# A pair of modulation units on the second value unit, and a ScalarE copy ahead of the gMLP's norm

## The chip, the cores and the metric

The kernel is one program on one of the eight cores of a Trainium2 chip. A core has five engines with a queue each: TensorE (PE, with its weight loads shown apart as PEld), VectorE (DVE), ScalarE (ACT), GpSimd (POOL) and SyncE (SP). Here SP issues nearly all transfers, and POOL and ACT issue a few. The metric is device time in microseconds (us), the median of several runs.

## The reference, cut to what matters

One encoder layer is run on 1024 frames of a new stream and 32 frames of a running one, so 1056 rows of 1024 features. Everything is float32. In outline:

```
mod = silu(c) @ w_ada + b_ada                  # sh1, sc1, g1, sh2, sc2, g2
h   = x * (1 + sc1) + sh1
mq mk mv mo mi mf | fq fk fv ff | gu gv = split(h @ w_in)
hm  = mLSTM(mq, mk, mv, mi, mf), normed, times sigmoid(mo)
hf  = forgetting attention(fq, fk, fv, ff)
vn  = layer_norm(gv, gmlp_ln_g, gmlp_ln_b)      # over 256 features
hg  = gu * (tril(ws) @ vn + bs)
x   = layer_norm(ALPHA * x + (1 + g1) * (concat(hm, hf, hg) @ w_o))
h   = x * (1 + sc2) + sh2
x   = layer_norm(ALPHA * x + (1 + g2) * ((silu(h @ w_gate) * (h @ w_up)) @ w_down))
```

The outputs are y, the attention's k, v and log forget values, the mLSTM's final states, and for the running stream `vn`. Two things matter here: the columns of `mod` (the adaLN modulation, a product of one vector with a 1024 x 6144 matrix) and `vn`.

## The kernel before, in words

**Arithmetic.** A float32 product is made of three fast ones: each operand is split into a rounded part (`hi`) and the rest (`lo`), and TensorE forms hi·hi, hi·lo and lo·hi. The split of a weight tile is a copy on ScalarE (line 117) and a subtraction on VectorE or GpSimd (line 118). A weight tile of 512 KB comes into one of three `raw` buffers.

**The adaLN units.** `w_ada` is cut into 24 units of 256 columns, two loads of 512 KB each. `ada_parts` (lines 193 to 215) takes a list of units. For each it issues 8 narrow matmuls (four k-tiles in four row groups, two halves), which the chip's trace shows as 16 records; the units of one list use different rows of the same accumulation. Then, once for a list, there is one ScalarE copy of the bank (line 206, tile `ada_adas`), two transposes (line 211) and one VectorE reduction (line 213); and for each unit the two or three small VectorE operations of `ada_end`. Units 16 to 19 make g1, which is first read when the output projection is evacuated, far later.

Units 0 to 7 are worked in the first stage. Units 16 and 17 are worked as a list of two by `group`: their four loads go into the pool `pe` (tag `early`, `EB` = 4 buffers), and their work is put after the first row tile of the second value unit. Units 18, 19 and then 8 to 15 are in the list `rest`, which `more(n)` works off singly, with the pool `pl` (tag `late`, 2 buffers, so the two loads of a unit wait until the unit before has been read). `T1[3]` = 2 says that two of them, 18 and 19, are put after the first part of the gates; each `a` in the string `ORDER` takes one more.

**The value units.** `tm_unit` (line 389) multiplies all rows with 264 or 256 columns. It first does the 32 sample rows (`sample_tile`, line 409), then eight tiles of 128 rows, each of 24 matmuls (lines 402 to 404) into one of the three banks of the pool `pg` (tag `g`). The evacuation of a value tile is `evac_v`: a ScalarE copy from the bank to `traw` (line 434, two buffers), a store of it to `o_v` by SP, VectorE copies and a split into `vhl` (lines 437 to 441, two buffers), and a store of that to `dv` by SP. A bank is free once its line 434 has run, and that waits until the store from the same `traw` buffer, two tiles back, has landed.

**The gMLP's gate tiles.** In `ORDER`, `G0` and `G2p` are `tm_unit` on the gv columns, for row tiles 0 to 3 and 4 to 8, with `evac_gv` (line 468) for each tile; `G1p` and `G3` are the gu columns with `evac_gmlp`. `evac_gv` reads the bank twice on VectorE: for the statistics (lines 472, 473) and, after the reciprocal root (`rstd`: two ScalarE operations at lines 461 and 462, three VectorE ones at 464 to 466), for the normalising `tensor_scalar` (line 477) into `traw`. GpSimd then scales and shifts `traw` (lines 478, 479) and issues the store to `dvn`. A bank is held until line 477 is done.

**What sets the order.** The functions only list the work. A planner in the Tile framework puts it into the engines' queues by its own timeline: at each moment the earliest-listed instruction that is ready in that timeline goes first, so a load whose buffer is free is issued well ahead of its place in the code. Each queue then runs strictly in order. `tie` and `pinned` add order where the planner is not to choose; `group` ties TensorE's part of a list behind the last matmul before it. In the program, an SP transfer also waits for the eighth SP transfer before it, since eight completion semaphores are used in turn. Pools are laid out as a stack from both sides; `pe` lies on the right side, over memory that the first stage used and that `mx0` (the attention's, mLSTM's and gates' tiles) uses afterwards.

Of the kernel before, what the change touches and what calls it, by code (L numbers as in the profile page):

```python
# [7 lines left out]
F32 = mybir.dt.float32  # L8
# [7 lines left out]
P = 128  # L16
# [16 lines left out]
LWE = 1  # L33
NB = (3, 2, 2)
PRE = 5
EB = 4
T1 = (0, 0, 0, 2)
XB, AB = (3, 6)
HPA = 200
MLB = (1, 2, 3, 4, 5)  # L40
# [29 lines left out]
class Kernel:  # L70
# [396 lines left out]

    def evac_gv(self, tt, ps, n):
        nc = self.nc
        st = self.t(self.sm, [P, 6], F32, "bst", 2)  # L470
        mv = self.t(self.sm, [P, 2], F32, "bmv", 2)
        nc.vector.bn_stats(st[:n], ps[:n, :256])
        nc.vector.bn_aggr(mv[:n], st[:n])
        r = self.t(self.sm, [P, 1], F32, "brs", 2)
        self.rstd(r[:n], mv[:n, 1:2], self.eps5[:n], self.sm, "brt")
        v = self.t(self.sm, [P, 256], F32, "traw", 2)
        nc.vector.tensor_scalar(v[:n], ps[:n, :256], mv[:n, 0:1], r[:n], ALU.subtract, ALU.mult)  # L477
        nc.gpsimd.tensor_tensor(v[:n], v[:n], self.rowp[:n, 272:528], ALU.mult)
        nc.gpsimd.tensor_tensor(v[:n], v[:n], self.rowp[:n, 528:784], ALU.add)
        self.store(self.dvn[:n, tt, :], v[:n], nc.gpsimd)  # L480
        if tt == 8:
            self.store(self.d["o_vn"], v[:n])
# [1016 lines left out]
    def run(self):  # L1499
        nc, tc, d = self.nc, self.tc, self.d  # L1500
# [52 lines left out]
        sl = ExitStack()  # L1553
        self.pl = self.pada = self.pool("pl", ctx=sl)
        w1 = d["w_in_v"]
        rest = [18, 19] + list(range(8, 16))

        def more(n):
            for u in rest[:n]:
                self.ada((u,), self.pl, "late", 2, self.pt, "t")  # L1560
            del rest[:n]

        more(T1[0])
        se = ExitStack()
        pe = self.pool("pe", ctx=se, side="right")

        def group(units):
            def go():
                first = len(nc.cur_bb.bb.instructions)
                target = self.lastmm  # L1570
                for _ in self.ada_parts(units, raws, self.pt, "t"):
                    pass
                self.tie(nc.cur_bb.bb.instructions[first:], target, (mybir.EngineType.PE,))
                self.phase = "tm"
            raws = [self.ada_load(u, pe, "early", EB) for u in units]
            return go

        self.tm_unit(w1[0], 264, self.evac_v(0))
        self.tm_unit(w1[1], 264, self.evac_v(1), between={0: group((16, 17))})
        se.close()  # L1580
        s2 = ExitStack()
        self.mx = self.pool("mx0", ctx=s2)
        more(T1[2])
        gates = self.gates()
        next(gates)
        more(T1[3])
        self.foxbufs = (2, 2, 2, 2, 3)
# [278 lines left out]
```

## Time and profile before

| | |
|---|---|
| median of 3 runs | 1346.33 us (1344.91 to 1347.18) |
| the profiled execution: its time, its span | 1346.69 us, 1344.9 us |
| first stage (h and the first products) | 0 to 58 us |
| the two value units | 58 to 111 us |
| gates, heads, attention, mLSTM, gMLP | 111 to 345 us |
| the G0 and G2p tiles' norms | 263 to 279 us, 299 to 328 us |
| output projection, feed-forward, tail | 345 to 1345 us |

The profiled execution has 1.8 us around its span. A row of the timeline begins with its start and its length in us, then engine, source line, operation, written and read tiles; in brackets stands the idle time of the engine before it and what ended it. A row of the windows gives for each engine the busy us and in brackets the number of instructions, then the granted clock, the share of the DMA engines that was busy, and GB/s. A row of a source line gives the shortest, median and longest duration in ns.

### The profile page before, as it was taken

How to read it: one execution, taken by the hardware profiler on the slowest of the kernel's cores; microseconds unless marked ns; L12 is line 12 of the kernel's file. 1: busy time of each engine (PE TensorE's matmuls, PEld its weight loads, DVE VectorE, ACT ScalarE, POOL GpSimd, SP SyncE). 2: the span in 40 equal slices, each digit the busy share in tenths (PEclk: the TensorE clock that was granted, in tenths of full speed). 3: DMA queues.
4: the chain of work that ended last, by engine and by line, in shares of the span. 5: the costliest groups of instructions: out<-in, count | busy, mean ns of one | idle time of the engine just before them, and what ended most of it. 6: DMA issues, size and time to landing. Idle time of an engine off the chain costs nothing.

```text
span 1344.9 us, 25607 instructions
## 1 busy us (share of the span) xinstructions
PE 1324.0 (98%) x9684; PEld 1208.3 (90%) x9684; DVE 989.1 (74%) x2091; ACT 655.8 (49%) x1305; POOL 231.9 (17%) x263
## 2 busy tenths in 40 slices
PE   9999999999999999999999999999999999999996
PEld 6798888888999888888888888999999999999995
DVE  5635655678779667686876776678979887988777
ACT  3413445455547545545454454435754453635355
POOL 0102100143246100000000001464610000000341
PEclk9999999999999999999999999999999999999999
DMA  9585465546557754454344332663785858554221
GB/s 362 207 299 154 150 204 186 174 131 207 181 195 257 191 136 130 117 163 126 115 121 116 110 104 82 217 175 112 205 231 154 228 148 225 139 175 131 89 79 67
DMA packets 119450, 221.73 MB, mean 165 GB/s; under 512 B 18580, under 2 KB 62768, under 8 KB 119328
## 3 DMA queue, kind: packets, MB, share of 16 engines
q1 hardware_dynamic: 112096, 207.55, 49.0%
q0 software_dynamic: 6032, 11.94, 5.2%
q8 instruction: 76, 1.25, 0.4%
q10 hardware_dynamic: 1200, 0.62, 0.2%
q14 instruction: 46, 0.38, 0.1%
HBM read 188.13 MB, written 51.85 MB: 178 GB/s over the span
## 4 chain that ended last, share of the span: by engine, by line
PE 68%; DVE 4%; DMA 1%; ACT 1%; issue 1%; DVEq 0%; ACTq 0%
PE up_g L130 6%; PE up_g L132 6%; PE up_g L131 6%; PE dn_g L130 4%; PE dn_g L132 4%; PE dn_g L131 4%; PE sup_u L132 3%; PE sup_u L131 3%; PE sup_u L130 3%; PE wo_g L131 2%; PE wo_g L132 2%; PE wo_g L130 2%; PE sup_g L132 2%; PE sup_g L131 2%; PE sup_g L130 2%; PE fox_t L943 2%
## 5 line engine op out<-in xcount | busy, mean ns | idle before, releaser
L130 PE MATMUL up_g<-tm_ah,up_whi 128*128 128x512 f32 (+1 forms) x384 | 140.0, 365 | 0.0
L131 PE MATMUL up_g<-tm_al,up_whi 128*128 128x512 f32 (+1 forms) x384 | 140.0, 365 | 0.0
L132 PE MATMUL up_g<-tm_ah,up_wlo 128*128 128x512 f32 (+1 forms) x384 | 139.7, 364 | 0.0
L1368 ACT CAST sup_whi<-sup_raw 128x1024 fp32r<-128x1024 f32 x54 | 56.1, 1048 | 89.3 <-PE dn_u L131 43.9
L130 PEld LDWEIGHTS up_g<-tm_ah,up_whi 128*128 128x128 f32 x384 | 72.3, 188 | 11.1 <-DVE tm_al L1246 0.4
L132 PEld LDWEIGHTS up_g<-tm_ah,up_wlo 128*128 128x128 f32 x384 | 72.3, 188 | 11.1
L131 PEld LDWEIGHTS up_g<-tm_al,up_whi 128*128 128x128 f32 x384 | 72.3, 188 | 10.7
L916 ACT ACTIVATE fox_p<-fox_s,fox_fmx 128x384 f32<-128x384 f32 (+2 forms) x96 | 55.2, 579 | 53.0 <-DVE fox_fmx L914 41.2
L1199 DVE SCALAR_TENSOR_TENSOR wo_z<-dn_g,start_mod,wo_z 128x512 f32<-128x512 f32 (+4 forms) x120 | 60.3, 521 | 22.6 <-PE dn_g L132 22.0
L118 DVE TENSOR_TENSOR up_wlo<-up_raw,up_whi 128x1024 fp32r<-128x1024 f32 x50 | 65.2, 1305 | 15.0 <-ACT up_whi L117 13.7
L1369 DVE TENSOR_TENSOR sup_wlo<-sup_raw,sup_whi 128x1024 fp32r<-128x1024 f32 x54 | 68.0, 1263 | 10.7 <-ACT sup_whi L1368 10.7
L117 ACT CAST up_whi<-up_raw 128x1024 fp32r<-128x1024 f32 x50 | 52.4, 1048 | 47.2 <-PE up_g L131 23.9
L130 PE MATMUL dn_g<-up_acth,dn_whi 128*128 128x512 f32 (+2 forms) x200 | 73.5, 368 | 0.8 <-DVE wo_z L1199 0.8
L132 PE MATMUL dn_g<-up_acth,dn_wlo 128*128 128x512 f32 (+2 forms) x200 | 73.3, 366 | 0.0
L131 PE MATMUL dn_g<-up_actl,dn_whi 128*128 128x512 f32 (+2 forms) x200 | 72.8, 365 | 0.0
L948 ACT CAST fox_pth<-fox_t 128x512 fp32r<-128x512 f32 (+1 forms) x80 | 41.6, 542 | 59.2 <-PE fox_t L943 57.5
L117 ACT CAST dn_whi<-dn_raw 128x1024 fp32r<-128x1024 f32 (+1 forms) x44 | 42.7, 971 | 51.7 <-PE up_g L131 16.0
L911 DVE TENSOR_REDUCE fox_fmx<-fox_s 128x1 f32<-128x384 f32 (+2 forms) x96 | 52.8, 553 | 16.3 <-PE fox_s L908 15.0
L949 DVE TENSOR_TENSOR fox_ptl<-fox_t,fox_pth 128x512 fp32r<-128x512 f32 (+1 forms) x80 | 49.9, 631 | 15.9 <-ACT fox_pth L948 15.6
L118 DVE TENSOR_TENSOR dn_wlo<-dn_raw,dn_whi 128x1024 fp32r<-128x1024 f32 (+1 forms) x44 | 49.5, 1125 | 10.4 <-ACT dn_whi L117 9.5
L402 PE MATMUL tm_g<-tm_whi,start_h1h 128*128 128x256 f32 (+1 forms) x192 | 55.3, 288 | 0.7 <-DVE tm_traw L477 0.7
L1320 POOL DMA_DIRECT2D start_dp<-w_gu x19 | 19.8, 1067 | 209.0 <-DMA start_dp<-w_gu 209.0
(684 smaller groups left out, 4799.7 us busy)
## 6 DMA issues: line engine op xcount, KB each, us to landing
up_raw<-w_gu SPq DMA_DIRECT2D x50, 512.0 KB
ada_late<-w_ada SPq DMA_DIRECT2D x28, 512.0 KB
dn_raw<-w_dn SPq DMA_DIRECT2D x28, 512.0 KB
sup_raw<-w_gu SPq DMA_DIRECT2D x20, 512.0 KB
start_dp<-w_gu SPq DMA_DIRECT2D x19, 512.0 KB
start_dp<-w_gu POOLq DMA_DIRECT2D x19, 512.0 KB, 8.0
wo_raw<-w_o SPq DMA_DIRECT2D x18, 512.0 KB
sup_raw<-start_dp SPq DMA_DIRECT2D x18, 512.0 KB
```

The lines of the kernel that those rows point to most:

```text
L117: nc.scalar.copy(hi[:, :w], raw[:, :w])
L118: (eng or nc.vector).tensor_tensor(lo[:, :w], raw[:, :w], f(hi[:, :w]), ALU.subtract)
L130: nc.tensor.matmul(ps, hi, xh(k), start=start and k == 0, stop=False)
L131: nc.tensor.matmul(ps, hi, xl(k), start=False, stop=False)
L132: self.lastmm = nc.tensor.matmul(ps, lo, xh(k), start=False, stop=stop and k == n - 1)
L402: nc.tensor.matmul(ps[:, :ncol], xh, hi, start=k == 0, stop=False)
L911: nc.vector.tensor_reduce(mxs[:, x:x + 1], s[:, :w], AX.X, ALU.max, negate=True)
L916: nc.scalar.activation(pr[:, lo:hi], banks[x][:, :hi - lo], AF.Exp, bias=mxs[:, 0:1], accum_out=sums[:, x:x + 1])
L949: nc.vector.tensor_tensor(pl[:, :e], ps[:, :e], f(ph[:, :e]), ALU.subtract)
L1199: self.lastz = self.nc.vector.scalar_tensor_tensor(z[:, m, x:y], ps[:, x - a:y - a], g[i], z[:, m, x:y], ALU.mult, ALU.add)
L1368: nc.scalar.copy(h, x)
L1369: tt(l, x, f(h), ALU.subtract)
```

## The change

Two things are done. First, units 18 and 19 leave `rest` and become a list of two, like 16 and 17. Its loads are listed in the code right after the first pair's work, after the first row tile of the second value unit, and its work after that unit's sixth row tile (number 5). `EB` becomes 8, so that the second pair has four buffers of its own; `T1[3]` becomes 0. With that, `rest` begins at unit 8, and the two `late` buffers are first used by unit 8. Second, `evac_gv` takes its `traw` tile at the start; for row tiles 0 to 7 ScalarE copies the bank into it, and the statistics and the `tensor_scalar` read the copy; the `tensor_scalar` writes the copy in place. Tile 8 (the sample rows) is as before.

```diff
-EB = 4
-T1 = (0, 0, 0, 2)
+EB = 8
+T1 = (0, 0, 0, 0)
...
     def evac_gv(self, tt, ps, n):
         nc = self.nc
+        v = self.t(self.sm, [P, 256], F32, "traw", 2)
+        if tt < 8:
+            nc.scalar.copy(v, ps[:, :256])
+            ps = v
         st = self.t(self.sm, [P, 6], F32, "bst", 2)
...
         self.rstd(r[:n], mv[:n, 1:2], self.eps5[:n], self.sm, "brt")
-        v = self.t(self.sm, [P, 256], F32, "traw", 2)
         nc.vector.tensor_scalar(v[:n], ps[:n, :256], mv[:n, 0:1], r[:n], ALU.subtract, ALU.mult)
...
-        rest = [18, 19] + list(range(8, 16))
+        rest = list(range(8, 16))
...
         self.tm_unit(w1[0], 264, self.evac_v(0))
-        self.tm_unit(w1[1], 264, self.evac_v(1), between={0: group((16, 17))})
+        pairs = [group((16, 17))]
+        self.tm_unit(w1[1], 264, self.evac_v(1), between={
+            0: lambda: (pairs[0](), pairs.append(group((18, 19)))), 5: lambda: pairs[1]()})
```

## The prediction

> **What bounds the kernel.** I read the head of the page first, then the windows, then what TensorE waited for between 55 and 420 us, then the timelines around the changed places.
>
> ```profile
> span 1344.9 us, 25607 instructions
> PE 1324.0 (98%) x9684; PEld 1208.3 (90%) x9684; DVE 989.1 (74%) x2091; ACT 655.8 (49%) x1305; POOL 231.9 (17%) x263
> ```
>
> TensorE is busy 1324.0 of 1344.9 us, so nothing can win more than the 20.9 us in which it is not, plus work taken off it. The windows of the changed stages (busy us by engine, clock, DMA share, GB/s):
>
> ```profile
> 58.00:110.00 52.00, 51.21 (x545) 49.62 (x545) 18.31 (x66) 11.77 (x32) 0.00 (x0) 1.00 0.78 264
> 140.00:260.00 120.00, 118.90 (x1010) 104.02 (x1009) 73.31 (x201) 62.99 (x155) 4.22 (x7) 1.00 0.54 167
> 260.00:280.00 20.00, 19.45 (x142) 18.05 (x141) 14.23 (x33) 7.58 (x16) 11.15 (x13) 1.00 0.55 186
> 300.00:330.00 30.00, 28.30 (x275) 25.81 (x264) 25.38 (x80) 14.31 (x40) 12.87 (x19) 1.00 0.56 178
> ```
>
> TensorE lost 0.8 us in the value units, 1.1 in 120 us after them, 0.55 and 1.7 where the gate tiles' norms are. The waits name each loss (engine, line, releaser: total, times, longest):
>
> ```profile
> PE fox_o L951 <- DVE fox_ptl L949: 1.1, 1, 1.1
> PE tm_g L416 <- DVE tm_traw L477: 1.0, 1, 1.0
> PE tm_g L416 <- ACT tm_traw L434: 0.7, 1, 0.7
> PE tm_g L402 <- DVE tm_traw L477: 0.7, 1, 0.7
> PE tm_g L402 <- DVE tm_brt L464: 0.6, 1, 0.6
> ```
>
> Three of these are a bank held by the norm (L477 twice, and L464, an operation of the same chain), together 2.3 us. One, 0.7 us, is a bank of the value units that ScalarE had not yet copied. Every us won or lost here moves the end by a us, since TensorE is full afterwards.
>
> **Part 1, TensorE's work for units 18 and 19.** A single unit in the timeline of before (its matmuls, then its transposes), and the pair 16/17:
>
> ```profile
> 131.23 0.29 PE L130 MATMUL fm_g<-start_h1h,gates_whi 128*128 128x272 f32 x1
> 131.45 1.07 PE L202 MATMUL ada_t<-ada_late,start_c 128*32 128x256 f32 x16
> 132.45 0.40 PE L131 MATMUL fm_g<-start_h1l,gates_whi 128*128 128x272 f32 x1
> 132.68 0.28 PE L132 MATMUL fm_g<-start_h1h,gates_wlo 128*128 128x272 f32 x1
> ```
>
> ```profile
> 135.33 0.29 PE L132 MATMUL fm_g<-start_h1h,gates_wlo 128*128 128x272 f32 x1
> 135.46 0.38 PE L211 MATMUL ada_t<-start_ident,ada_adas 128*128 128x128 f32 x2
> 135.59 0.38 PE L130 MATMUL fm_g<-start_h1h,gates_whi 128*128 128x272 f32 x1
> 135.80 0.28 PE L131 MATMUL fm_g<-start_h1l,gates_whi 128*128 128x272 f32 x1
> ```
>
> ```profile
> 87.80 0.28 PE L404 MATMUL tm_g<-tm_whi,start_al 128*128 128x264 f32 x1
> 88.01 1.93 PE L202 MATMUL ada_t<-tm_early,start_c 128*32 128x256 f32 x32
> 89.88 0.39 PE L402 MATMUL tm_g<-tm_whi,start_ah 128*128 128x264 f32 x1
> 90.11 0.29 PE L403 MATMUL tm_g<-tm_wlo,start_ah 128*128 128x264 f32 x1
> ```
>
> Matmuls follow each other at about 0.13 us (135.33 to 135.46). From 131.23 to 132.68 are 1.45 us for two such steps and the unit's matmuls: 1.45 - 0.26 = 1.19. Its two transposes: 135.80 - 135.33 - 0.26 = 0.21. Two single units: 2 x 1.40 = 2.80. The pair: 90.11 - 87.80 - 0.26 = 2.05, plus one set of transposes 0.21 = 2.26. **Saved 0.54 us**, as much for the second change of tile shape as for the transposes. All of it is on the path, for TensorE has no pause around either place. The ScalarE copy and reduction saved (one each) are off the path, as is `ada_end`, whose count stays: g1 is read 200 us later. Bounds: 0.6 won; or 1.1 lost, if the single units were filling a gap at 131 and 141 us that a stall like fox_o's (1.1) takes. I take -0.54, the measured rows.
>
> **Part 2, the loads, and the value units' stores.** Here the change can cost. In SP's queue, loads are issued as soon as buffers allow:
>
> ```profile
> 68.35 1.29 SPq L87 DMA_DIRECT2D tm_early<-w_ada  x2
> 70.93 0.34 SPq L91 DMA_DIRECT2D o_v<-tm_traw  x1
> 71.32 1.19 SPq L87 DMA_DIRECT2D tm_early<-w_ada  x2
> 72.62 0.51 SPq L91 DMA_DIRECT2D start_dv<-tm_vhl  x1
> 73.19 1.23 SPq L87 DMA_DIRECT2D ada_late<-w_ada  x2
> 74.76 0.37 SPq L91 DMA_DIRECT2D o_v<-tm_traw  x1
> ```
>
> ```profile
> 76.46 0.38 ACT L434 COPY tm_traw<-tm_g 128x264 f32<-128x264 f32 x1 [4.68 <-DMA o_v<-tm_traw]
> 83.20 0.38 ACT L434 COPY tm_traw<-tm_g 128x264 f32<-128x264 f32 x1 [6.37 <-DMA o_v<-tm_traw]
> ...
> 84.46 0.38 ACT L434 COPY tm_traw<-tm_g 128x264 f32<-128x264 f32 x1
> ...
> 85.68 0.39 ACT L434 COPY tm_traw<-tm_g 128x264 f32<-128x264 f32 x1
> ```
>
> ```profile
> 80.24 0.29 DVE L440 CAST tm_vhl<-tm_traw 128x256 fp32r<-128x256 f32 x1 [3.20 <-DMA start_dv<-tm_vhl]
> 83.64 1.13 PE L416 MATMUL tm_g<-tm_raw,start_hs 128*32 128x66 f32 x64 [0.66 <-ACT tm_traw L434]
> ```
>
> The store issued at 74.76 stands behind six loads and lands at 83.2: 8.4 us, in which ScalarE's sixth copy waits, and TensorE for its bank. The rate: from the landing at 76.46 (store of 70.93) to the one at 80.24 (72.62) two 512 KB loads and a 256 KB store arrive, 1.31 MB in 3.8 us; a load is about 1.45 us.
>
> After the change, the pair 18/19 wants four loads and unit 8 two, as the two `late` buffers are free from the start; before, only unit 18's two were issued here. So four loads (5.8 us) are new in this stretch. Two of the pair's take the places of 73.19. For the other four loads I expect the next free places: one between the stores that follow 74.76 and the copy at 84.46, which moves to about 85.5, and three ahead of the store that the copy at 85.68 waits for, which moves to about 91. TensorE then waits for the bank of 84.46, +1.0, and begins the second unit's second tile at 90.9 instead of 89.88, where the bank of the last copy is 0.5 late: **+1.5 us** in all. Later copies have two tiles (5.8 us at 24 x 0.12) of slack, and the loads of v for the heads now wait for the second pair's memory, which eases the queue behind. The end below is -0.7 (the existing 0.66 goes too, if the stores land earlier), the end above +5.8 (all four ahead of the store of 74.76). I take +1.5, since a store that is ready precedes a load listed after it in the planner's order. The pair's work at tile 5, some 15 us after its last load, waits for nothing.
>
> **Part 3, the gate tiles.** Eight ScalarE copies are added, and eight VectorE operations change their source:
>
> ```profile
> L452 ACT COPY tm_traw<-tm_g x16: 362/372/376, 172.6 to 256.6; 128x256 f32<-128x256 f32 x16
> L477 DVE TENSOR_SCALAR tm_traw<-tm_g,tm_bmv,tm_brs x8: 528/544/545, 265.6 to 323.8; 128x256 f32<-128x256 f32 x8
> ```
>
> The copies are 8 x 0.372 = 3.0 us of ScalarE, which is busy 7.58 of 20 and 14.31 of 30 us there: hidden. VectorE's `tensor_scalar` may fall from 0.544 towards the 0.29 of the cast at 80.24, which reads and writes SBUF, 2 us at most, hidden too. What counts is when the bank comes free: after one copy, not after statistics, two ScalarE and five VectorE operations. Of the 2.3 us I take **-2.0**: a bank that the copy frees some us earlier isn't waited for, but the copies now hold `traw` (two buffers) from the copy until the store to `dvn` has landed, and a copy that waits for it stops ScalarE, and behind it the weight casts of line 117, for which the splits on VectorE and GpSimd and then TensorE's next unit wait. Those casts are what is late next. Bounds: -2.3 (all three waits) to +1.5 (three tiles' ScalarE stops of 0.5 us, the size of the waits that go).
>
> **The sum.** -0.54 + 1.5 - 2.0 = -1.0 us against the profiled execution's 1346.7: 1345.7. That execution is 0.4 above the median of the runs shown, so 1345.3 as a median, within 0.2% (2.7 us, about what a measurement of this kernel can tell from no change; its three runs spread over 2.3).
>
> **Rivals** (as medians).
> *Slower: all new loads ahead of the waiting store.* Place: between 71 and 76 us. If the planner puts the four before the store of 74.76, the copy of 83.20 comes at 89.0 and TensorE's 0.66 becomes 6.5: -2.54 + 5.8 = +3.3, 1349.6. It decides once all but a fraction of one load is ahead (5.2 us needed to pass +2.7). For it: nothing but buffers holds loads back; against: a ready store goes first.
> *Faster: the stores stay ahead.* Parts 1 and 3 whole and the 0.66 gone: -0.54 - 2.3 - 0.66 = -3.5, 1342.8; with the 0.66 kept, 1343.5. For it: DMA is busy only 0.78 of the stage.
> *The copy moves the wait.* ScalarE stalls on `traw` for as much as the bank wait was: part 3 is 0, sum +1.0, 1347.3.
> *The planner shifts the rest.* Between 110 and 260 us TensorE lost 1.1 us in one stall; other queue orders can hardly win there, but four new stalls of that size give +4.4 - 1.0 = +3.4, 1349.7.
> *VectorE is held by GpSimd.* Beside a weight split of GpSimd, a 0.16 us operation took 2.72:
>
> ```profile
> 273.33 2.72 DVE L465 SCALAR_TENSOR_TENSOR tm_brt<-tm_brt,tm_brs 128x1 f32<-128x1 f32 x1
> ```
>
> If two of the eight `tensor_scalar`, now from memory to memory, are held 2.5 us each and half of that reaches TensorE through the weight splits, -1.0 + 2.5 = +1.5, 1347.8. [...]
>
> **How the numbers follow.** The forecast 0.32; stores ahead 0.22; copy moves the wait 0.14; loads ahead 0.14; planner 0.13; held VectorE 0.05. The forecast's own range is 1343.8 to 1347.0. Faster by over 0.2%: 0.22 and a sliver of the forecast, 0.25. Slower: the two rivals at 1349.6 and 1349.7, 0.28 with the upper reaches of the others. Within: 0.47. The range reaches from the faster case's 1342.8 to past the slower ones, 1350.2.
>
> **What would show it.** Right: one 32-record group of units 18 and 19 near 107 us, and none near 131 and 141; TensorE's wait for L434 1 to 2 us at 84 to 91; no wait on L477 or L464; a wait of ScalarE for the `dvn` store. Wrong: a wait for L434 above 4 us, or none; TensorE idle over 2 us between 110 and 260; casts of line 117 in 265 to 330 that TensorE waits for; the new `tensor_scalar` above 1 us.

## The result, and the profile after

The changed kernel takes 1351.6 us against 1346.24 for the kernel before, 1.0040 times as long (95% interval 1.0031 to 1.0050); beside it on another chip 1350.85 against 1346.4, 1.0030 (1.0020 to 1.0041). The forecast was 1345.3, with a range to 1350.2: the change is slower, by 4.5 to 5.4 us, and beyond the range. Three executions of the kernels below, one each of e3_held, e8b_copy48 and e10_held_copy_act, took 1430, 7389 and 2162 us and are left out of every time, ratio and count. The changed kernel's profiled execution took 1353.02 us, 6.3 more than that of before. The head of its page:

```profile
span 1351.2 us, 25608 instructions
PE 1327.4 (98%) x9682; PEld 1211.6 (90%) x9682; DVE 988.6 (73%) x2090; ACT 658.5 (49%) x1312; POOL 228.9 (17%) x263
```

TensorE has two instructions less, and is busy 3.4 us *more*; its idle time grew by 2.9 (1351.2 - 1327.4 = 23.8, before 20.9). Fewer instructions that take longer point to the clock, the seventh column of the windows (busy us of PE, PEld, DVE, ACT, POOL, then clock, DMA share, GB/s):

```profile
82.00:88.00 6.00, 3.14 (x79) 2.76 (x78) 2.65 (x4) 3.02 (x7) 0.00 (x0) 0.96 1.03 412
88.00:94.00 6.00, 6.00 (x56) 4.92 (x55) 1.60 (x8) 0.87 (x3) 0.00 (x0) 0.75 1.03 411
140.00:260.00 120.00, 119.55 (x992) 105.69 (x991) 71.97 (x197) 61.59 (x151) 6.67 (x11) 1.00 0.53 161
260.00:280.00 20.00, 20.00 (x152) 18.16 (x152) 11.11 (x28) 8.51 (x19) 10.19 (x11) 1.00 0.58 178
300.00:330.00 30.00, 29.10 (x278) 26.38 (x276) 24.38 (x79) 15.66 (x47) 11.28 (x18) 1.00 0.57 185
330.00:340.00 10.00, 9.51 (x62) 8.02 (x61) 8.93 (x28) 7.36 (x22) 1.56 (x2) 0.83 0.94 284
380.00:390.00 10.00, 7.76 (x64) 7.42 (x63) 8.47 (x9) 3.24 (x5) 6.49 (x10) 1.00 0.58 194
```

The gate tiles' stretches won 1.35 us of the 2.0 forecast (0.55 lost in 260 to 280 is now 0; 1.70 in 300 to 330 is now 0.90), and between 140 and 260 us 0.45 is lost instead of 1.1. The value units lose 2.9 us in 82 to 88 (before 0.8) and then run six us at a mean clock of 0.75. And there are two losses where none was looked for: a low clock at 330 to 340 (0.83 over 10 us, 1.7 us), and 2.2 us at 380 to 390, in the output projection. The waits of TensorE in 55 to 420 us name them:

```profile
PE wo_g L130 <- DVE wo_z L1202: 2.5, 3, 1.2
PE tm_g L402 <- ACT tm_tmsum L420: 1.5, 1, 1.5
PE tm_g L416 <- ACT tm_traw L434: 1.3, 1, 1.3
PE mlstm_s L765 <- DVE tm_brt L465: 0.9, 1, 0.9
```

(Lines from 477 on stand three lower down than in the kernel before: L477 is L480, L1199 is L1202.) No wait for the norm's bank is left.

**In the value units**, this is SP's queue, and below it ScalarE's:

```profile
75.27 0.38 SPq L91 DMA_DIRECT2D o_v<-tm_traw  x1
76.47 0.33 SPq L87 DMA_DIRECT2D tm_early<-w_ada  x1
76.89 0.66 SPq L91 DMA_DIRECT2D start_dv<-tm_vhl  x1
79.27 0.33 SPq L87 DMA_DIRECT2D tm_early<-w_ada  x1
80.52 0.98 SPq L87 DMA_DIRECT2D ada_late<-w_ada  x2
82.46 0.34 SPq L91 DMA_DIRECT2D o_v<-tm_traw  x1
```

```profile
76.92 0.38 ACT L434 COPY tm_traw<-tm_g 128x264 f32<-128x264 f32 x1 [4.20 <-DMA o_v<-tm_traw]
84.14 0.38 ACT L434 COPY tm_traw<-tm_g 128x264 f32<-128x264 f32 x1 [6.84 <-DMA o_v<-tm_traw]
...
86.33 0.86 ACT L420 COPY tm_tmsum<-tm_g 32x66 f32<-32x66 f32 x4
90.72 0.38 ACT L434 COPY tm_traw<-tm_g 128x264 f32<-128x264 f32 x1 [3.53 <-DMA o_v<-tm_traw]
91.47 0.38 ACT L434 COPY tm_traw<-tm_g 128x264 f32<-128x264 f32 x1 [0.36 <-DMA o_v<-tm_traw]
```

The tile copied at 76.92 is stored only at 82.46, behind four loads. Its buffer is the one the copy of 90.72 needs: before, the copy in this place came at 84.46. So two of the three banks are held until 91, the second unit has only the sample tile's bank to go on with, and TensorE waits 1.5 us for that as well. The loads hold that store up chiefly in SP's queue. From the end of its copy (77.30) to its issue are 5.2 us, and for 3.5 of them SP waits for earlier loads to land before it can issue the next transfer; in before the store of this tile was issued at once (76.87). From issue to landing it then takes 8.3 us, in before at most 7.6.

What the clock then does is seen in the distance of matmuls and in windows of one us:

```profile
88.07 0.42 PE L403 MATMUL tm_g<-tm_wlo,start_ah 128*128 128x264 f32 x1
88.29 0.42 PE L404 MATMUL tm_g<-tm_whi,start_al 128*128 128x264 f32 x1
```

```profile
87.00:88.00 1.00, 0.76 (x4) 0.76 (x5) 1.00 (x1) 0.19 (x1) 0.00 (x0) 0.77 1.00 410
88.00:89.00 1.00, 1.00 (x7) 1.00 (x6) 0.72 (x4) 0.00 (x0) 0.00 (x0) 0.50 1.01 394
89.00:90.00 1.00, 1.00 (x6) 1.00 (x6) 0.00 (x0) 0.00 (x0) 0.00 (x0) 0.50 1.07 402
90.00:91.00 1.00, 1.00 (x7) 1.00 (x6) 0.00 (x0) 0.28 (x1) 0.00 (x0) 0.53 1.07 433
91.00:92.00 1.00, 1.00 (x12) 0.86 (x15) 0.83 (x4) 0.48 (x2) 0.00 (x0) 1.00 1.00 410
```

It is 0.22 us from one matmul to the next instead of 0.13, until 90.9. By the windows the clock is at one half for some 3.4 us; one minus the clock, summed over them, is 1.7 us. Such a stretch is called a fall below. Ahead of this one TensorE had two gaps, of 1.31 and 1.55 us, with 1.1 us of work between them.

**In the output projection**, rows of the timeline of before, and then of after:

```profile
371.62 0.50 DVE L492 SCALAR_TENSOR_TENSOR fm_qkl<-fm_g,start_qsc,fm_qkh 128x272 fp32r<-128x272 f32 x1 [1.69 <-DMA start_dql<-fm_qkl]
376.25 7.58 POOL L1193 TENSOR_TENSOR wo_z<-wo_z,wo_pv 128x256 f32<-128x256 f32 x7 [2.22 <-ACT wo_pv L1057]
378.46 0.45 DVE L1071 TENSOR_TENSOR wo_zs<-wo_z 128x256 f32<-128x256 f32 x1
```

```profile
377.49 1.22 DVE L118 TENSOR_TENSOR wo_wlo<-wo_raw,wo_whi 128x1024 fp32r<-128x1024 f32 x1 [3.05 <-ACT wo_whi L117]
378.63 0.49 DVE L495 SCALAR_TENSOR_TENSOR fm_qkl<-fm_g,start_qsc,fm_qkh 128x272 fp32r<-128x272 f32 x1
379.26 1.62 POOL L499 TENSOR_TENSOR fm_qkr<-fm_qkh,fm_qkl 128x272 f32<-128x272 f32 x1 [5.46 <-ACT wo_pv L1060]
381.90 4.89 POOL L1196 TENSOR_TENSOR wo_z<-wo_z,wo_pv 128x256 f32<-128x256 f32 x7
382.67 0.48 DVE L1202 SCALAR_TENSOR_TENSOR wo_z<-wo_g,start_mod,wo_z 128x256 f32<-128x256 f32 x1 [1.50 <-POOL wo_z L1196]
383.19 3.88 DVE L1074 TENSOR_TENSOR wo_zs<-wo_z 128x256 f32<-128x256 f32 x1
386.99 0.47 DVE L1202 SCALAR_TENSOR_TENSOR wo_z<-wo_g,start_mod,wo_z 128x256 f32<-128x256 f32 x1
```

The planner, with another list in front of it, has put the last early head's split (`fm_qkl`, one tile of 272 columns) behind a weight split, which itself waits 3.05 us for ScalarE's cast. GpSimd's addition for that head then comes after `wo_pv` is there instead of 4 us before it, and holds back the seven subtractions from z, which GpSimd does next: they begin 3.0 us after `wo_pv` was begun, in before 0.5. VectorE waits 1.5 us for the first of them. Then its sum of z takes 3.88 us instead of 0.45, until GpSimd is through; the evacuation behind it comes late, and TensorE waits for the bank. From the first to the last matmul of the output projection (rows of its tile in before and after):

```profile
L130 PE MATMUL wo_g<-tm_ah,wo_whi x128: 278/281/468, 366.9 to 413.8; 128*128 128x256 f32 x128
```

```profile
L130 PE MATMUL wo_g<-tm_ah,wo_whi x128: 277/281/469, 370.2 to 420.4; 128*128 128x256 f32 x128
```

46.9 us became 50.2. This length, "the projection's length" below, and TensorE's loss in 82 to 88 us tell in each experiment which of the two is there. The length is the surer sign: the loss in 82 to 88 varies from 0 to 2.74 in kernels that have before's loads.

### The profile page after: what moved, and what is told of

Its sections match the earlier page's. It is cut to its first block, busy times and chain, and to the rows that moved or that the text cites. A ratio compares the mean times of both kernels' runs of the same rounds, so it can differ in the third digit from the quotient of the medians.

```text
span 1351.2 us, 25608 instructions
## 1 busy us (share of the span) xinstructions
PE 1327.4 (98%) x9682; PEld 1211.6 (90%) x9682; DVE 988.6 (73%) x2090; ACT 658.5 (49%) x1312; POOL 228.9 (17%) x263
## 4 chain that ended last, share of the span: by engine, by line
PE 65%; DVE 4%; DMA 4%; ACT 2%; issue 2%; SPq 0%; POOL 0%; DVEq 0%; ACTq 0%; POOLq 0%
PE up_g L130 6%; PE up_g L132 6%; PE up_g L131 6%; PE dn_g L130 4%; PE dn_g L132 4%; PE dn_g L131 4%; PE sup_u L132 3%; PE sup_u L131 3%; PE sup_u L130 3%; PE wo_g L130 2%; PE sup_g L132 2%; PE sup_g L131 2%; PE wo_g L132 2%; PE wo_g L131 2%; PE sup_g L130 2%; PE fox_t L946 2%
## 5 line engine op out<-in xcount | busy, mean ns | idle before, releaser
L1202 DVE SCALAR_TENSOR_TENSOR wo_z<-dn_g,start_mod,wo_z 128x512 f32<-128x512 f32 (+4 forms) x120 | 60.1, 519 | 22.3 <-PE dn_g L132 21.6
L402 PE MATMUL tm_g<-tm_whi,start_ah 128*128 128x256 f32 (+1 forms) x192 | 55.7, 291 | 1.5 <-ACT tm_tmsum L420 1.5
```

Source lines behind the costliest of these rows:

```text
L402: nc.tensor.matmul(ps[:, :ncol], xh, hi, start=k == 0, stop=False)
L1202: self.lastz = self.nc.vector.scalar_tensor_tensor(z[:, m, x:y], ps[:, x - a:y - a], g[i], z[:, m, x:y], ALU.mult, ALU.add)
```

## The experiments

All ratios are to the kernel before on the same chip. "Clock low" counts the executions whose mean granted clock was 0.996 or less; of the kernel before that were 34 of 119. In the 17 profiled executions that mean is 0.997 or 0.998 where there is no fall ahead of the kernel's last 12 us, 0.996 where there is one (r_after, e4_late8held, e9_traw4, e13_after_act), and 0.995 with the two of the change.

| kernel | time, before (us) | ratio (95%) | TensorE lost in 82 to 88 | projection's length | clock low |
|---|---|---|---|---|---|
| the change | 1351.6, 1346.24 | 1.0040 (1.0031 to 1.0050) | 2.86 | 50.2 | 4 of 6 |
| r_after, the same again | 1350.85, 1346.4 | 1.0030 (1.0020 to 1.0041) | 2.08 | 50.0 | 6 of 7 |
| e1_pair | 1347.22, 1345.65 | 1.0013 (1.0002 to 1.0024) | 2.54 | 47.1 | 4 of 10 |
| e2_copy | 1348.81, 1345.65 | 1.0021 (1.0010 to 1.0032) | 1.03 | 50.4 | 3 of 10 |
| e3_held | 1346.84, 1345.65 | 1.0005 (0.9989 to 1.0020) | 0 | 49.3 | 1 of 9 |
| r_e3_held, the same again | 1346.8, 1346.4 | 1.0005 (0.9996 to 1.0014) | 0.28 | 49.8 | 2 of 11 |
| e4_late8held | 1350.95, 1345.65 | 1.0038 (1.0026 to 1.0051) | 2.93, and 1.00 in 88 to 94 | 50.5 | 8 of 10 |
| e6_pair_held | 1344.84, 1346.33 | 0.9992 (0.9981 to 1.0004) | 0.84 | 46.9 | 4 of 10 |
| e7_copy_act | 1345.27, 1346.33 | 0.9997 (0.9986 to 1.0009) | 0 | 47.5 | 3 of 10 |
| e8b_copy48 | 1344.47, 1346.33 | 0.9991 (0.9979 to 1.0003) | 0.17 | 46.9 | 1 of 9 |
| e9_traw4 | 1346.73, 1346.33 | 1.0005 (0.9995 to 1.0014) | 0 | 46.9 | 5 of 10 |
| e10_held_copy_act | 1344.72, 1346.1 | 0.9988 (0.9977 to 0.9998) | 0.71 | 47.9 | 2 of 11 |
| e11_held_copy48 | 1344.57, 1346.1 | 0.9989 (0.9980 to 0.9999) | 0.55 | 46.9 | 2 of 12 |
| e12_before_act | 1347.1, 1346.1 | 1.0008 (0.9999 to 1.0017) | 2.74 | 48.3 | 2 of 12 |
| e13_after_act | 1346.49, 1346.1 | 1.0006 (0.9994 to 1.0019) | 3.82 | 47.9 | 5 of 12 |
| e14_after_fill | 1348.84, 1346.4 | 1.0020 (1.0011 to 1.0029) | 0 | 49.3 | 0 of 11 |

### One part of the change at a time

The pair alone is the changed kernel with the old `evac_gv`; the copy alone is the kernel before with the new one.

> The pair of units 18 and 19 alone, with the gate tiles' norm as it was before (no ScalarE copy). Theory A (the pair's four loads and unit 8's two go ahead of the value units' stores): the value units lose what they lost in the changed kernel, 2.07 us of idle TensorE in 58 to 110 us and the granted clock of 0.75 behind it (about 1.6 us), part 1 wins 0.54, the gate tiles' 2.3 us of waits stay, nothing new in 330 to 420: 1346.2 + 3.1 = about 1349.4 us. Theory B (the loss comes with the ScalarE copy, in the output projection at 380 to 391 us): 1345.7, the value units as before. Theory C (any new order of the planner costs, wherever it is): the stall of 2.5 us at 380 to 391 is there without the copy too, above 1351.

> The gate tiles' ScalarE copy alone, with units 18 and 19 loaded and computed singly as before. Theory A (all of the loss is the loads): 2.0 us faster than before, 1344.2, with no wait on the norm's bank and no new wait in 330 to 420. Theory B (the copy costs later): the waits on the norm's banks are gone (1.4 to 2.0 us won), but the output projection's stall of 2.5 us at 380 to 391 and the low clock at 333 to 337 (0.83 over 10 us, 1.7 us) are there: 1346.2 - 2.0 + 4.2 = about 1348.4. Theory C as in e1_pair.

Theory A holds for the pair (the stall is there, the projection is as before; it is 1.6 us slower, about half of the 3.1 expected, and its profiled execution has no fall of the clock) and fails for the copy: the copy alone is 2.8 us slower, close to the 1348.4 of theory B. Its projection takes 50.4 us, and TensorE has the same kind of wait there, with none left on the norm's bank. The low clock that theory B had at 333 to 337 is not in its profile (1.00 in 330 to 340). Theory C, that any new order costs, is out: the pair's order differs from that of before, too, but on GpSimd it is the same to the instruction, and its projection takes 47.1.

### The loads held back

```diff
-            self.store(self.dv[...], f(hl).rearrange(...))
+            st = self.store(self.dv[...], f(hl).rearrange(...))
+            if half == 0:
+                self.laststore = st
...
         def more(n):
             for u in rest[:n]:
-                self.ada((u,), self.pl, "late", 2, self.pt, "t")
+                with tc.issue_after(self.laststore.ins) if u == 8 else ExitStack():
+                    raws = self.ada_load(u, self.pl, "late", 2)
+                for _ in self.ada_parts((u,), [raws], self.pt, "t"):
+                    pass
...
-            raws = [self.ada_load(u, pe, "early", EB) for u in units]
+            with tc.issue_after(self.laststore.ins) if units[0] == 18 else ExitStack():
+                raws = [self.ada_load(u, pe, "early", EB) for u in units]
```

`issue_after` puts these loads behind the first value unit's last store to `dv` in SP's queue. e3_held is the whole diff on the changed kernel; e4_late8held has all but the last three lines; e6_pair_held is e3_held with the old `evac_gv`.

> The changed kernel, with the loads of units 18 and 19 and of unit 8 held on SP's queue until the first value unit's last store to dv has been issued. Theory A: the sixth copy's store is no longer behind six or more loads, the value units lose at most before's 0.8 us, the clock stays at 1.00: 1351.6 - 3.6 = about 1348.0, and what is left over 1346.2 is the output projection. Rival (the stall is the store's own time and not the loads ahead of it): 1351.6, with a stall of 2 us where it was.

> The changed kernel, with only unit 8's two loads held behind the first value unit's last store to dv; the pair's four loads stay where they were. If every load ahead of the stores counts alike (1.45 us each), a third of the loss goes: the copy that waited 3.53 us until 90.72 comes about 2.9 us earlier, 1351.6 - 1.2 = about 1350.4. If the pair's four alone make the stall: 1351.6, no change. If unit 8's two alone make it: as e3_held, about 1348.0.

> The pair alone, its loads and unit 8's held until the first value unit's last store to dv has been issued; the gate tiles' norm as before, no copy. Theory (the value units' loss is the loads ahead of the stores, and nothing else costs): no TensorE wait in 58 to 110, part 1's 0.54 and the 0.8 us of before's value units won, 1345.65 - 1.3 = about 1344.3; against the pair with its loads not held (1347.2) 2.9 less. Rival (the pair costs by itself, through the second unit's matmul order or the later loads): no faster than the pair alone, 1347 or above.

The windows of e3_held and of e4_late8held at the place:

```profile
82.00:88.00 6.00, 6.00 (x110) 5.33 (x112) 4.38 (x12) 3.65 (x9) 0.00 (x0) 1.00 0.71 244
```

```profile
82.00:88.00 6.00, 3.07 (x80) 2.68 (x79) 1.61 (x4) 2.10 (x3) 0.00 (x0) 1.00 1.02 398
88.00:94.00 6.00, 5.00 (x36) 4.68 (x40) 3.27 (x10) 1.68 (x7) 0.00 (x0) 0.72 0.77 237
```

With all six loads held the stall is gone, and some 4 us with it (1350.85 against 1346.8 on one chip). With unit 8's two alone held nothing is gained: the pair's four loads are enough for the stall. Without the copy, the held pair is 1.1 us (by the ratio) below before, as its theory had it (1.3), though the interval takes in no change; against the pair not held it wins 2.8 (1.0013 to 0.9992), where 2.9 was expected.

### GpSimd's late start

```diff
         for h in range(QD, PRE):
-            self.fm_unit(w3[1 + h], self.evac_qk(h), (1,))
+            self.fm_unit(w3[1 + h], self.evac_qk(h, h == PRE - 1), (1,))
```

For this one head, `evac_qk` then lets ScalarE copy k and the sample columns from the bank and issue the store, so that GpSimd has nothing ahead of its subtractions. e7_copy_act is this on the copy alone, e12_before_act on the kernel before, e13_after_act on the changed kernel. In the last, TensorE's, VectorE's and SP's orders are those of the changed kernel but for one instruction of VectorE that has moved.

> The copy alone, and the last early head's k is written by ScalarE from the bank, so that GpSimd's addition (1.62 us, finished at 377.65) and its store no longer stand ahead of GpSimd's subtractions from z. Theory G (GpSimd's late subtractions make the loss at the output projection: VectorE waits 1.5 us for them, and its sum of z is held 3.87 us beside them): they start at about 376.0 as before instead of 378.67, the waits of wo_g on wo_z go (1.5 us), the stage from first to last wo_g falls from 50.4 to about 47.5, and the time from 1348.8 to about 1346. Rival (the stage is late because the weights' casts and loads of wo are in another order): 50.4 stays, 1348.8.

> The kernel before with the last early head's k written by ScalarE, and nothing else: the control for the two kernels that have this edit. If it only takes away what the copy's new order brought: no change, 1346.0 plus or minus 0.7, with a wo_g stage of 46.9 us. If the edit wins by itself: 1345 or below, and its gain must be taken off the others'.

> The changed kernel with the last early head's k written by ScalarE; loads as they were. If the output projection's loss is GpSimd's late start: the wo_g stage falls from 50.2 to about 47.3, 1351.6 - 3.0 = about 1348.3, and what is left is the value units' stall and the low clock behind it. Rival (VectorE is held wherever GpSimd subtracts): 50.2 stays, 1351.

VectorE and GpSimd in e13_after_act (the groups of their source lines in 370 to 395 us, with the shortest, median and longest ns and the first and last start):

```profile
L1074 DVE TENSOR_TENSOR wo_zs<-wo_z x1: 425/425/425, 382.3 to 382.3; 128x256 f32<-128x256 f32 x1
```

```profile
L1196 POOL TENSOR_TENSOR wo_z<-wo_z,wo_pv x7: 725/923/1720, 380.8 to 386.7; 128x256 f32<-128x256 f32 x7
```

GpSimd begins 0.5 us after `wo_pv` was begun, the sum of z takes 0.43 us again, and the projection 47.9. The copy alone goes from 1.0021 to 0.9997, the changed kernel from 1.0030 to 1.0040 down to 1.0006, though its value units still stall (3.82 us in the profiled execution). The control excludes that the edit wins by itself: on the kernel before it costs 1.0 us, if anything (its projection is 48.3 us, where 46.9 was expected). In the seven profiled executions with the addition in front (the change, r_after, e2, e3, r_e3, e4 and e14) the sum of z takes 3.85 to 3.89 us and the projection 49.3 to 50.5; in the ten others 0.42 to 0.46 and 46.9 to 48.3. So the late start is the cause of the projection's loss, and not the weights' order, which stayed.

### The copy on half the tiles

```diff
-        if tt < 8:
+        if 4 <= tt < 8:
```

> The ScalarE copy for the second gate unit's tiles 4 to 7 alone; tiles 0 to 3 as before. If what costs in the copy is the new order that the first four tiles bring to the output projection (GpSimd's and SP's order are before's here but for two lines each): the wo_g stage is 46.9 us as before, the 1.7 us of waits at 320 to 330 go, 1345.65 - 1.7 = about 1344.0. If the copies themselves cost (ScalarE stopped for the store to dvn, ahead of the weight casts): half of the 2.8 us loss, about 1347.

Here the planner leaves the projection as it was (46.9), and the time is 1.2 us below before by the ratio, though the interval takes in no change. The four copies show no cost of their own, and neither do all eight once the late start is away (e7_copy_act, 0.9997).

### More buffers instead of later loads

```diff
-            raw = self.t(self.sm, [P, 264], F32, "traw", 2)
+            raw = self.t(self.pe, [P, 264], F32, "vraw", 4)
...
-        pe = self.pool("pe", ctx=se, side="right")
+        pe = self.pe = self.pool("pe", ctx=se, side="right")
```

> The pair alone with its loads where they were, but the value units' copies have four buffers instead of two, in the second pair's memory. Theory A (the copy waits for a buffer whose store is behind the loads): ScalarE's wait at 84 is gone, TensorE does not wait in the value units, about 1344.3 to 1345 against 1347.2. Rival (DMA bandwidth itself is what is short): the wait moves to another transfer, the store to dv or the next weights, and 1347 stays.

This settles only in part what it should. The loss in 82 to 88 is gone with the loads where they were, though the DMA engines are as full there as in the changed kernel (a share of 1.04, there 1.03): DMA as full as that did not by itself stop TensorE here. But these buffers lie in memory that the first stage used, and ScalarE's first copies now wait, until 70.50:

```profile
PE tm_g L402 <- ACT tm_vraw L434: 2.3, 1, 2.3
```

That wait lies ahead of 82 us, and with it the clock falls as well (0.93 over 58 to 82 us, again 1.7 us). At 0.4 us above before, the time stands between the two theories.

### Idle time or clock

```diff
         self.tm_unit(w1[0], 264, self.evac_v(0))
+        def fill(n):
+            dps = self.t(self.pt, [P, 512], F32, "t")
+            first, target = len(nc.cur_bb.bb.instructions), self.lastmm
+            for i in range(n):
+                nc.tensor.matmul(dps[:, :256], self.h1parts(0, P)[0](0), self.h1parts(0, 256)[0](0),
+                                 start=i == 0, stop=i == n - 1)
+            self.tie(nc.cur_bb.bb.instructions[first:], target, (mybir.EngineType.PE,))
+        fill(20)
+        self.fill = fill
```

The second call, `fill(12)`, stands in `sample_tile` after its matmuls.

> The changed kernel with 32 extra matmuls, which compute nothing that is used: 20 of them (2.5 us) after the first value unit's last tile, 12 (1.5 us) after the second unit's sample tile, where TensorE waits 1.3 and 1.5 us. If the low clock behind the stall follows from TensorE's idle time: the granted clock stays at 1.00 in 82 to 100 us, the executions with a clock of 0.994 to 0.996 become as rare as in the kernel before, and although up to 1.2 us of work is added the median falls by 0.5 to 2 us below the changed kernel's on this chip. If the clock falls for another reason: the same dips, and 0 to 1.2 us slower.

> The changed kernel once more, beside the kernel before on one chip. If its loss was rightly measured: 1.0040 times before, 5.4 us, of which the executions with a clock of 0.997 or more have about 3.5 and those below 6 to 7. If the two causes add (3.0 for GpSimd's late work, 2.5 for the loads, less 1.5 won): 4.0 us, 1.0030.

> The changed kernel with its loads held once more: without the stall, most executions have a clock of 0.997 or more, and the difference to the changed kernel on the same chip is 2.5 us if the stall's idle time is all, 4 to 5 if the low clock behind it counts as much again.

The windows of r_after and of e14_after_fill:

```profile
82.00:88.00 6.00, 3.92 (x82) 3.54 (x82) 3.14 (x6) 3.02 (x7) 0.00 (x0) 0.90 1.03 409
88.00:94.00 6.00, 6.00 (x58) 4.92 (x57) 1.33 (x7) 1.13 (x3) 0.00 (x0) 0.81 1.05 411
```

```profile
82.00:88.00 6.00, 6.00 (x106) 5.77 (x105) 3.15 (x6) 3.12 (x7) 0.00 (x0) 1.00 1.01 399
88.00:94.00 6.00, 6.00 (x67) 4.93 (x66) 2.05 (x9) 1.14 (x3) 0.00 (x0) 1.00 0.86 300
```

The loads and ScalarE's waits are those of the changed kernel, but TensorE multiplies through them, to no use. Not one of 11 executions has a low clock, against 10 of the changed kernel's 13, and with some 4 us of work added where 2 to 3 us were idle the median is 2.0 us lower (1348.84 against 1350.85; 1.3 by the ratios). So the clock falls at this place because TensorE is idle. A fall is not of the stall's size: every one in the profiles costs 1.7 us, behind 2.1 us of idle time as behind 3.9. To win 1.3 to 2.0 us while 1 to 2 us of work are added takes, as an estimate from these numbers, more than one fall in the median execution; two are seen in one profile alone, that of the change (at 87 and at 333 us). In the changed kernel's 13 executions the median is 1349.5 at a clock of 0.997 or more (three of them) and 1351.6 below.

### Both causes away

> The changed kernel with both causes taken away: the loads held behind the first value unit's last store to dv, and the last early head's k written by ScalarE. If the two causes are all of it and add: the pair held alone is 1.1 to 1.5 faster than before, the copy with k on ScalarE 0.6 to 1.0, together 1.7 to 2.5: about 1344.0 against 1346.0. If a third cost is in the combination: 1346 or above.

> The pair with its loads held, and the copy for the gate tiles 4 to 7 alone, GpSimd's work as it was. If the gains add (1.1 to 1.5 and 1.2 to 1.4): 2.3 to 2.9 faster than before, about 1343.4. If the gate tiles' waits only pass to later ones: as the pair held alone, 1344.8.

By the ratios both are faster than before by 1.5 to 1.6 us, with intervals that just leave out no change, and 5.5 us or more below the changed kernel. e10 did not reach its 1344.0, and e11 not its 1343.4: the gains of the held pair (1.1) and of the half copy (1.2) come to 1.5 together, which the intervals do not tell from their sum.

## Why the prediction was wrong

**Part 1** was right in its rows. The pair, in the timeline of after, takes 110.87 - 108.57 - 0.26 = 2.04 us for its matmuls (forecast 2.05). Whether its 0.54 us reach the end was not measured alone: the 1.1 of e6_pair_held take in more, and no change lies in their interval.

```profile
108.57 0.28 PE L404 MATMUL tm_g<-tm_whi,start_h1l 128*128 128x264 f32 x1
108.78 1.93 PE L202 MATMUL ada_t<-tm_early,start_c 128*32 128x256 f32 x32
110.64 0.39 PE L402 MATMUL tm_g<-tm_whi,start_h1h 128*128 128x264 f32 x1
110.87 0.29 PE L403 MATMUL tm_g<-tm_wlo,start_h1h 128*128 128x264 f32 x1
```

**Part 2** had the mechanism and was mis-sized: +1.5 forecast, and in the profiled execution 2.1 more idle (2.86 - 0.79) and 1.7 of clock. The step that failed is the place of the four new loads, "one between the stores that follow 74.76 and the copy at 84.46, ... and three ahead of the store that the copy at 85.68 waits for". All four went ahead of the store that the copy of 84.46 waits for. That copy moved to 90.72 and not to 85.5, and two banks were held instead of one. The reason given, "a store that is ready precedes a load listed after it", does not carry: in the queue the store of the tile copied at 76.92 stands behind them. Whether the planner's own timeline had that store ready later, no run shows. The rival with all loads ahead of the waiting store put them one store too early (the copy of 83.20 only moved to 84.14). No term was there for the clock, since the profile of before shows it at 1.00 in every window quoted; how much the stall varies by itself is seen with before's loads: e7_copy_act lost nothing there, before 0.79, e12_before_act 2.74.

**Part 3** was right where it looked and wrong as a sum. The bank comes free early, none of the three waits of 2.3 us is left, and both edited lines are as short as forecast (after, groups of the two lines):

```profile
L472 ACT COPY tm_traw<-tm_g x8: 356/373/374, 265.8 to 321.8; 128x256 f32<-128x256 f32 x8
L480 DVE TENSOR_SCALAR tm_traw<-tm_traw,tm_bmv,tm_brs x8: 400/412/414, 268.8 to 327.7; 128x256 f32<-128x256 f32 x8
```

At 0.414 us at most, no `tensor_scalar` was held by GpSimd: the rival "VectorE is held by GpSimd" did not come true at the instruction it was put on. It was not put to the test there, for in the trace none of the eight runs beside a GpSimd operation on tiles, and their rows (0.400 to 0.414 us) show nothing of the 2.5 us it gave to each of two. Nor were the casts of line 117 waited for by TensorE. ScalarE's new waits for a `traw` buffer were 4.5 us for the store to `o_vn`, once, and 0.6 for `dvn`, and no wait of TensorE names them; two new waits there, 0.9 for `tm_brt` and 0.4 for `head_k`, took back a part. What failed is the sentence "those casts are what is late next", with the upper bound of +1.5 taken from the same stage. What was late next lay some 55 us behind the last gate tile: one head's split, GpSimd's subtractions, and VectorE held beside them, 3.3 us in the projection. The rival "the planner shifts the rest" had the mechanism's first half, but was searched for in 110 to 260 us only and priced by fox_o's stall. None of the prediction's signs of being wrong came up: they too lay only where a loss was looked for.

**The sum.** By the ratios of the runs and not by one profile: removing the stall is worth 3.4 us (r_after against r_e3_held; 4.0 by their medians), 2.4 to 2.8 where the other cause is away or absent (e13_after_act against e10_held_copy_act, e1_pair against e6_pair_held); removing GpSimd's late start is worth 2.3 to 4.6 (e3 to e10, e2 to e7, the change to e13); and without both the change wins 1.6, against the forecast's -0.54 - 2.0 = -2.5 for parts 1 and 3. Within their intervals of about 1.5 us each these add to the 4.5 to 5.4 measured. Whether the two causes make each other worse is not settled, and neither is the low clock at 330 to 340 in the first profiled execution, for which those of r_after, e2_copy and e4_late8held show no counterpart, and ahead of which TensorE was idle for only 0.5 us (330 to 332).

## What to carry to other kernels

When an edit frees buffers early, write out the queue up to the first store whose landing an evacuation waits for, and count every load that can stand ahead of it: holding six loads behind the stores won back some 4 us. A planner's order can break far behind the edited lines, so compare the engines' orders over the whole program, GpSimd's first where it shares work with VectorE. Price a stall of TensorE of 2 to 4 us at its length, and at 1.7 us more for the fall of the clock that came with it in five profiled executions here.

## What the runs showed of the hardware

Ahead of the last 12 us of the kernel, five of the 17 profiled executions have falls of the granted clock, six in all. The two of the change go to 0.50 and cost 1.70 us each by windows of one us, so about 3.4 us at half rate; the other four cost 1.7 us each by wider windows (r_after 0.84 and 0.99 over 80 to 90 and 90 to 100 us, e13_after_act 0.89 and 0.94, e4_late8held 0.72 over 88 to 94, e9_traw4 0.93 over 58 to 82). The idle time differed: gaps of TensorE of 0.54 and 1.55 us (r_after), 1.31 and 1.55 (the change), 2.28 and 1.54 (e13_after_act), 2.39 and 1.55 (e4_late8held), each pair with 1.1 us of narrow matmuls between, or 2.26 alone (e9_traw4); the sixth is that at 333 us. In the 11 executions in which matmuls of no use filled the gaps, the mean clock was never below 0.997. The fall does not follow each time: 0.99 and 1.54 us (e1_pair) and 2.61 alone (e12_before_act) left the clock at 1.00. Of the executions of e13_after_act, whose profile has the stall, 5 of 12 have a low clock, and they are the five slowest (1349.4 to 1351.9, the others 1344.1 to 1346.5); whether the others had the stall is not known. What decides was not found.

VectorE's sum of z (`tensor_tensor`, 128x256) took 3.88 us in the changed kernel, from 383.19 to 387.07, beside GpSimd's row of seven operations of 0.72 to 0.74 us each, from 381.90 to 386.79. In before it took 0.45 us while the same seven were under way; there these took 0.91 to 1.72 us each, 7.58 us in all in place of 4.89. What decides between the two was not tried.
